# Moving the scatter of an expert unit's results into the next unit's products

## The chip, the core and the metric

The kernel runs on one core of a Trainium2 chip. The metric is the device time of one execution in microseconds (us). The engines are named as the profile names them: PE is the matrix engine (PEld its weight loads), DVE the vector engine, ACT the scalar engine, POOL the general engine, SP the queue that issues the transfers.

## What is computed

Two layers of a decoder trunk over 256 tokens of width 1024. Each layer has a mixing part (an RWKV head group and a sparse attention head group) and then a mixture of 16 experts, of which each token uses two. Only the second part is touched here. Its core, cut from the reference:

```python
h2 = rms_norm(x, norm_g[l, 1]) * (1.0 + sc2) + sh2
x = x + gate_ffn * moe_ffn(h2, router_w, router_b, exp_w_gate[l], exp_w_up[l], exp_w_down[l])

def expert_block(args):          # inside moe_ffn: xe are the tokens of expert e
    xe, e = args
    return (jax.nn.silu(xe @ w_gate[e]) * (xe @ w_up[e])) @ w_down[e]

yb = lax.map(expert_block, (xb, blk_expert)).reshape(P, D)
y = jnp.zeros((N + 1, D), h.dtype).at[slot_tok].add(yb * slot_w[:, None])
```

Each expert has 1024x512 gate weights, as many up weights and 512x1024 down weights in float32.

## The kernel before

The mixture is worked off in seven units per layer. A unit has 128 slots, shared between two experts of 64 slots (units 0, 1, 4, 5, 6), four experts of 32 (unit 2), or one of 96 and one of 32 (unit 3). A unit's products for its experts go to different column groups of the matrix engine (`tile_position` 0, 32, 64, 96: its lanes), so that neighbouring instructions of different lanes run at the same time.

The weights come in chunks of 1 MB, 96 per layer, in the order unit, matrix (gate, up, down), half of the contraction, expert. Counted from 0, unit 2 has chunks 24 to 47, unit 3 has 48 to 59, unit 4 has 60 to 71, unit 5 has 72 to 83, unit 6 has 84 to 95. `fetch` issues them on SP into a ring of 18 buffers, and a chunk can be issued when the chunk 18 places before it has been used.

The steps of a unit `i`:

- `pick` and `gather` (L1243, L1247): products of the token rows with one-hot columns bring the tokens of a pair of units into `xeA` or `xeB`; 32 products with full weights, for units 2 and 3 together, 4 and 5 together, and 6 alone.
- `prepare` (L1296, L1286, L1288, L1290): the one-hot matrix `ohT` that carries the unit's slots back to tokens, and the slots' weights `sw`.
- `hidden` (L1353): the gate products into one bank `pg`, then the up products into `pu`. For each, 8 steps of the contraction times the lanes.
- `gated` (L1306 on ACT, L1307 and L1308 on DVE): silu(gate) times up into `hb`.
- `turn` (L1315 on PE, L1317 on ACT): four transposes.
- `down` (L1364): the down products into two banks `p2[0]`, `p2[1]`, the two halves of the 1024 outputs.
- `scatter` (L274, L275, L1326, L1329), once for each half: ACT copies the half to `ys` in the reduced format, DVE writes the remainder (L275), PE multiplies both by `ohT` (eight products with full weights into `ps_rw`), DVE adds the result to `xT` (L1329). `ys` has one buffer, so the second half is copied when the first half's products have read it.

Before, unit `i`'s two scatters are issued in the program right behind `down(i)`, `pick` and `prepare(i+1)`, and a scheduler, which sets the order of each engine's queue when the kernel is built, lays them among the neighbouring instructions, those of `hidden(i+1)` among them. Ahead of the last unit's `turn` stands `rest`, a branch that is taken when an expert has more tokens than slots; every engine passes it.

Of the kernel before, what the change touches and what calls it, by code (L numbers as in the profile page):

```python
# [21 lines left out]
NK = D // 128  # L22
# [89 lines left out]
def tile_trunk(ctx: ExitStack, tc: tile.TileContext, a: dict, layers=L, dump=None):  # L112
    nc = tc.nc
    ve, ac, po, pe, sp = nc.vector, nc.scalar, nc.gpsimd, nc.tensor, nc.sync
# [183 lines left out]
    with tc.tile_pool(name="start", bufs=8, reuse_waits="tile") as start:  # L298
# [6 lines left out]
        pss = ps("sq")  # L305
# [4 lines left out]
        for ci in (2, 0, 3, 1):  # L310
            p = ps("mm")
# [7 lines left out]
            p = ps("rw")  # L319
# [8 lines left out]
    for l in range(layers):  # L328
# [740 lines left out]
        def fetch(n=0):  # L1069

            done[0] += n
            while len(loaded) < min(done[0] + len(slots), len(chunks)):
                i = len(loaded)
                e, m, r = chunks[i]
                w = slots[i % len(slots)].tile([128, 2048], F32, name="w", tag="w")
                sp.dma_start(w, a["exp"][l, expert(e), m, r])
                loaded[chunks[i]] = w
# [224 lines left out]
        def gated(p_g, p_u, sw, h):  # L1302

            for i in range(2):
                o = slice(256 * i, 256 * i + 256)
                ac.activation(h[:, o], p_g[:, o], AF.Tanh, scale=0.5)  # L1306
                ve.scalar_tensor_tensor(h[:, o], h[:, o], 1.0, p_g[:, o], op0=ALU.add, op1=ALU.mult)  # L1307
                ve.scalar_tensor_tensor(h[:, o], p_u[:, o], sw, h[:, o], op0=ALU.mult, op1=ALU.mult)  # L1308
# [10 lines left out]
        def scatter(p, cols, pss=None, store=False):  # L1319

            split(ys[:, 0], ys[:, 1], p)
            for j in range(0, len(cols), 2):
                p = ps("rw")
                for i, (d, o, ohT) in enumerate(cols[j:j + 2]):
                    for n in range(2):
                        pe.matmul(p[:, i * 256:i * 256 + 256], lhsT=ys[:, n, o:o + 128], rhs=ohT, start=(n == 0), stop=(n == 1),  # L1326
                                  skip_group_check=True)
                for i, (d, o, ohT) in enumerate(cols[j:j + 2]):
                    ve.scalar_tensor_tensor(xT[:, d, :], p[:, i * 256:i * 256 + 256], gfh[:, d:d + 1], xT[:, d, :],  # L1329
                                            op0=ALU.mult, op1=ALU.add)  # L1330
                    if store:
                        sp.dma_start(a["out"][:, d, :], xT[:, d, :])
                    if pss is not None:
                        sumsq(pss, d, xes[0][:, d, :])
# [9 lines left out]
        def hidden(i):  # L1344
            xe = xes[(i // 2) % 2]
            pg, pu = ps("mm"), ps("mm")
            for m, p in ((0, pg), (1, pu)):
                for r in range(2):
                    for k in range(4 * r, 4 * r + 4):
                        for e, o, n in lanes(i):  # L1350
                            w = loaded[e, m, r].rearrange("p (k n) -> p k n", k=4)
                            x = 128 * (i % 2) + o
                            pe.matmul(p[o:o + n, :], lhsT=xe[:, k, x:x + n], rhs=w[:, k % 4, :],  # L1353
                                      start=(k == 0), stop=(k == NK - 1), skip_group_check=True)
                    fetch(len(units[i]))
            gated(pg, pu, sws[i % 2], hs)

        def down(i, hsT):
# [56 lines left out]
        def sort():  # L1415

            key = mt([16], "key")
            ve.scalar_tensor_tensor(key, num, 16.0, C[:, C_KEY:C_KEY + 16], op0=ALU.mult, op1=ALU.add)
            t = hb[:, 512:1280].rearrange("p (a b c) -> p a b c", a=4, b=12)
            t2 = t.rearrange("p a b c -> p (a b c)")[:, 0:256].rearrange("p (a b) -> p a b", a=16)  # L1420
            ve.tensor_tensor(t2, key.unsqueeze(1).to_broadcast([128, 16, 16]), key.unsqueeze(2).to_broadcast([128, 16, 16]),
                             op=ALU.is_lt)
            rank = mt([16], "rank")
            ve.tensor_reduce(rank, t2, axis=AX.X, op=ALU.add)
            perm = hs[:, 128:320].rearrange("p (a b) -> p a b", a=12)
            ve.tensor_tensor(perm, rank.unsqueeze(1).to_broadcast([128, 12, 16]),
                             iota[:, 0:12].unsqueeze(2).to_broadcast([128, 12, 16]), op=ALU.is_equal)
            ve.tensor_mul(t[:, 0], perm, iota[:, 0:16].unsqueeze(1).to_broadcast([128, 12, 16]))
            ve.tensor_reduce(order_, t[:, 0], axis=AX.X, op=ALU.add)
            ve.tensor_copy(order, order_)  # L1430
            for x, o in ((rkp, 0), (wt, 2)):
                ve.tensor_mul(t[:, o:o + 2], x.unsqueeze(2).to_broadcast([128, 2, 12, 16]),
                              perm.unsqueeze(1).to_broadcast([128, 2, 12, 16]))
            ve.tensor_reduce(srt, t, axis=AX.X, op=ALU.add)

            ve.tensor_scalar(cap, rank, 4.5, -32.0, op0=ALU.is_lt, op1=ALU.mult)
            ve.tensor_scalar(key, rank, 11.0, 32.0, op0=ALU.is_equal, op1=ALU.mult)
            ve.scalar_tensor_tensor(cap, cap, 64.0, key, op0=ALU.add, op1=ALU.add)
            ve.tensor_sub(key, num, cap)
            ve.tensor_scalar(key, key, 0.0, None, op0=ALU.max)  # L1440
            ve.tensor_copy(over[:, 0:16], key)
            ve.tensor_reduce(rank[:, 0:1], key, axis=AX.X, op=ALU.max)
            ve.tensor_copy(over[:, 16:17], rank[:, 0:1])
# [6 lines left out]
        pick((0, 1), xes[0], lambda: [low_part(q) for q in range(1, 4)])  # L1450
        prepare(0)
        sort()
        for i in range(len(units)):
            last = i == len(units) - 1
            hidden(i)
            if last:
                if l + 1 < layers:
                    persist["win"] = {ci: load("win", l + 1, ci).rearrange("p (k n) -> p k n", k=NK) for ci in range(RA_N - 1)}
                rest(xes[1 - (i // 2) % 2])
            turn(hs, 128, hsTs[0])  # L1460
            p2 = down(i, hsTs[0])
            if last and l + 1 < layers:
                persist["win"][RA_N - 1] = load("win", l + 1, RA_N - 1).rearrange("p (k n) -> p k n", k=NK)
            if not last:
                if i % 2:
                    pick([j for j in (i + 1, i + 2) if j < len(units)], xes[((i + 1) // 2) % 2])
                prepare(i + 1)
            pss = ps("mm") if last and l + 1 < layers else None
            for n in range(2):
                scatter(p2[n], [(d, 128 * (d % 4), ohTs[i % 2]) for d in range(4 * n, 4 * n + 4)], pss,  # L1470
                        last and l + 1 == layers)
            if pss is not None:
                persist["rs"] = norm_rs(sumsq_end(pss, xes[0][:, 0, :]))
        E_.close()
# [76 lines left out]
```

## Time and profile before

| | us |
|---|---|
| three runs | 1196.7, 1196.71, 1189.7 |
| median | 1196.7 |
| profiled execution, its own time | 1189.87 |
| span of the profiled execution | 1188.1 |

| engine | busy, share of the span |
|---|---|
| PE | 90% |
| DVE | 55% |
| ACT | 34% |
| POOL | 11% |

The profiled execution is about as long as the fastest of the three runs, 6.8 us under their median. The mixture of layer 0 lies from about 380 to 617 us in the profile, that of layer 1 from about 950 us to the end, with the same pattern 571.9 us later. In the profile one product of float32 data (L1353, L1364) makes two rows of the count, so that x32 there are 16 instructions of the program; the products of the scatter and the gather (L1326, L1243) make one.

### The profile page before, as it was taken

To read this page: it belongs to the slowest core of one execution; us is meant where nothing else is said; L and a number is where in the kernel's file an instruction comes from. 1 tells how busy PE (TensorE), PEld (TensorE's weight loads), DVE (VectorE), ACT (ScalarE), POOL (GpSimd) and SP (SyncE) were. 2 spreads that over 40 slices of the span, in tenths; PEclk is the share of its full clock that TensorE was granted. 3 is DMA by queue.
4 is the path that set the end of the run, shared out by engine and by line. 5 is a ranking of instruction groups with operands and counts; after the bars stand their busy time and mean duration, and the time that the engine had idled before them with its cause. 6 is when DMAs were issued, how large, how long until landed. Compare 5 with 4: busy or idle time off the path is not lost. (4 is left out here: it accounts for less than half of the span.)

```text
span 1188.1 us, 19652 instructions
## 1 busy us (share of the span) xinstructions
PE 1068.4 (90%) x7568; PEld 688.4 (58%) x7568; DVE 653.2 (55%) x1727; ACT 402.8 (34%) x922; POOL 134.1 (11%) x196
## 2 busy tenths in 40 slices
PE   5779899998797999999968999999989799999996
PEld 2658767886696343333337777778769744333432
DVE  1799788788575322121238988886748532212222
ACT  1634434356553020101035444344655321120100
POOL 0431232310000000000023212331000000000000
PEclk9889999999798999999988899999999899999998
DMA  9755664474577999999775466433346969999991
GB/s 382 266 189 187 224 226 174 168 245 164 200 311 321 373 421 419 420 420 419 295 268 179 152 239 213 161 135 133 108 167 273 409 267 420 420 420 419 419 396 38
DMA packets 52815, 328.48 MB, mean 276 GB/s; under 512 B 5856, under 2 KB 7520, under 8 KB 18784
## 3 DMA queue, kind: packets, MB, share of 16 engines
q1 hardware_dynamic: 52416, 326.91, 70.5%
q8 instruction: 63, 1.03, 0.3%
q14 instruction: 48, 0.39, 0.1%
q10 hardware_dynamic: 288, 0.14, 0.0%
HBM read 325.98 MB, written 1.05 MB: 275 GB/s over the span
## 5 line engine op out<-in xcount | busy, mean ns | idle before, releaser
L288 PE MATMUL ps_mm<-h,w 128*128 128x256 f32 x1824 | 266.8, 295 | 16.4 <-ACT w L274 8.1
L288 PEld LDWEIGHTS ps_mm<-h,w 128*128 128x128 f32 x1824 | 233.5, 194 | 35.7 <-issue 10.1
L275 DVE TENSOR_TENSOR w<-w,w 128x1024 fp32r<-128x1024 f32 (+2 forms) x130 | 140.2, 1082 | 16.3 <-ACT w L274 16.1
L274 ACT ACTIVATE w<-w 128x1024 fp32r<-128x1024 f32 (+2 forms) x130 | 120.1, 936 | 61.4 <-PE ps_mm L288 36.7
L1353 PE MATMUL ps_mm<-w,xeA 128*64 128x512 f32 x512 | 130.1, 599 | 0.0
L1364 PE MATMUL ps_mm<-w,hb 128*64 128x512 f32 (+1 forms) x576 | 123.0, 607 | 1.7 <-DMA w<-in_exp 1.2
L225 DVE CUSTOM_DVE_ANT_0 wa<-wa,crow 128x1024 f32<-128x1024 f32 x80 | 98.3, 1229 | 1.2 <-DMA wa<-in_ada 1.0
L1353 PE MATMUL ps_mm<-w,xeB 128*32 128x512 f32 (+1 forms) x640 | 97.8, 595 | 0.0
L275 DVE TENSOR_TENSOR ys<-ps_mm,ys 128x512 fp32r<-128x512 f32 x28 | 19.2, 686 | 110.5 <-ACT ys L274 110.5
L1364 PEld LDWEIGHTS ps_mm<-w,hb 128*64 128x64 f32 (+1 forms) x576 | 36.6, 127 | 73.3 <-issue 66.3
L737 PE MATMUL ps_mm<-w,h 128*128 128x512 f32 (+1 forms) x288 | 76.2, 394 | 1.0 <-DVE w L275 0.7
L1353 PEld LDWEIGHTS ps_mm<-w,xeA 128*64 128x64 f32 x512 | 37.5, 137 | 65.6 <-issue 62.3
L1307 DVE SCALAR_TENSOR_TENSOR hb<-hb,ps_mm 128x256 f32<-128x256 f32 x28 | 11.8, 421 | 99.7 <-ACT hb L1306 99.7
L274 ACT ACTIVATE ys<-ps_mm 128x512 fp32r<-128x512 f32 x28 | 16.7, 596 | 131.2 <-PE ps_mm L1364 101.3
L1308 DVE SCALAR_TENSOR_TENSOR hb<-ps_mm,sw,hb 128x256 f32<-128x256 f32 x28 | 12.3, 480 | 86.5 <-PE ps_mm L1353 86.5
L1329 DVE SCALAR_TENSOR_TENSOR xT<-ps_rw,gfh,xT 128x256 f32<-128x256 f32 x112 | 46.6, 478 | 23.3 <-PE ps_rw L1326 23.3
L1353 PEld LDWEIGHTS ps_mm<-w,xeB 128*32 128x32 f32 (+1 forms) x640 | 26.0, 115 | 51.8 <-issue 48.4
L737 PEld LDWEIGHTS ps_mm<-w,h 128*128 128x128 f32 x288 | 48.1, 198 | 12.5 <-issue 2.7
L1326 PEld LDWEIGHTS ps_rw<-ohT,ys 128*128 128x128 f32 x224 | 30.6, 188 | 38.8 <-ACT ys L274 19.4
L1243 PEld LDWEIGHTS ps_rw<-OH,h 128*128 128x128 f32 x256 | 35.7, 208 | 29.7 <-issue 23.8
L288 PE MATMUL ps_mm<-y,w 128*128 128x256 f32 x384 | 49.8, 294 | 3.2 <-ACT w L274 3.0
L288 PEld LDWEIGHTS ps_mm<-y,w 128*128 128x128 f32 x384 | 48.9, 200 | 3.9 <-ACT w L274 3.8
(458 smaller groups left out, 1512.9 us busy)
## 6 DMA issues: line engine op xcount, KB each, us to landing
w<-in_exp SPq DMA_DIRECT2D x192, 1024.0 KB, 19.7
w<-in_win SPq DMA_DIRECT2D x40, 1024.0 KB, 4.9
wa<-in_ada SPq DMA_DIRECT2D x80, 512.0 KB, 4.5
w<-in_ada SPq DMA_DIRECT2D x8, 1024.0 KB, 14.1
w<-in_cmp SPq DMA_DIRECT2D x8, 1024.0 KB, 6.0
w<-in_up SPq DMA_DIRECT2D x8, 1024.0 KB, 7.1
w<-in_out SPq DMA_DIRECT2D x8, 1024.0 KB, 5.9
row<-in_row SPq DMA_DIRECT2D x2, 780.0 KB, 7.3
```

The costliest lines, as they stand in the source:

```text
L225: ve.tensor_tensor_reduce(w, w, crow, 1.0, 0.0, op0=ALU.mult, op1=ALU.add, accum_out=mod[:, o:o + 1])
L274: ac.activation(hi, x, AF.Copy)
L275: e.tensor_sub(lo, x, hi.bitcast(F32))
L288: pe.matmul(out, lhsT=w2[i][:, k, :], rhs=x2[j][:, k, :], start=(k == ks[0] and not (i or j)), stop=(k == ks[-1] and j == 1), skip_group_c ...
L737: pe.matmul(p[tt][:, 0:n], lhsT=h2[j][:, k, tt * 128:tt * 128 + 128], rhs=w2[i][:, k - k0, :], start=(k == 0 and not (i or j)), stop=(k == ...
L1243: pe.matmul(p[:, k * 256:k * 256 + n], lhsT=h[:, tt, kk_ * 128:kk_ * 128 + 128], rhs=OH[:, tt, 0:n], start=(i == 0 and tt == 0), stop=(i = ...
L1307: ve.scalar_tensor_tensor(h[:, o], h[:, o], 1.0, p_g[:, o], op0=ALU.add, op1=ALU.mult)
L1308: ve.scalar_tensor_tensor(h[:, o], p_u[:, o], sw, h[:, o], op0=ALU.mult, op1=ALU.mult)
L1326: pe.matmul(p[:, i * 256:i * 256 + 256], lhsT=ys[:, n, o:o + 128], rhs=ohT, start=(n == 0), stop=(n == 1), skip_group_check=True)
L1329: ve.scalar_tensor_tensor(xT[:, d, :], p[:, i * 256:i * 256 + 256], gfh[:, d:d + 1], xT[:, d, :], op0=ALU.mult, op1=ALU.add)
L1353: pe.matmul(p[o:o + n, :], lhsT=xe[:, k, x:x + n], rhs=w[:, k % 4, :], start=(k == 0), stop=(k == NK - 1), skip_group_check=True)
L1364: pe.matmul(p2[n][o:o + m, :], lhsT=hsT[:, 2 * r + g, o:o + m], rhs=w[:, g, n * 512:n * 512 + 512], start=(r + g == 0), stop=(r + g == 2), ...
```

## The change

The scatter of unit `i` is no longer issued behind `down(i)`. Its two halves are put on a list, and `hidden(i+1)` takes one from it behind its gate products and the other behind its up products. `tc.issue_after(mm.ins)` orders the half's products on PE behind the last of the products just issued. The last unit's halves are issued where they were.

```diff
                         for e, o, n in lanes(i):
                             w = loaded[e, m, r].rearrange("p (k n) -> p k n", k=4)
                             x = 128 * (i % 2) + o
-                            pe.matmul(p[o:o + n, :], lhsT=xe[:, k, x:x + n], rhs=w[:, k % 4, :],
-                                      start=(k == 0), stop=(k == NK - 1), skip_group_check=True)
+                            mm = pe.matmul(p[o:o + n, :], lhsT=xe[:, k, x:x + n], rhs=w[:, k % 4, :],
+                                           start=(k == 0), stop=(k == NK - 1), skip_group_check=True)
                     fetch(len(units[i]))
+                if behind:
+                    with tc.issue_after(mm.ins):
+                        behind.pop(0)()
             gated(pg, pu, sws[i % 2], hs)
...
+        behind = []
         for i in range(len(units)):
...
             pss = ps("mm") if last and l + 1 < layers else None
-            for n in range(2):
-                scatter(p2[n], [(d, 128 * (d % 4), ohTs[i % 2]) for d in range(4 * n, 4 * n + 4)], pss,
-                        last and l + 1 == layers)
+
+            def half(n, i=i, p2=p2, pss=pss, store=last and l + 1 == layers):
+                scatter(p2[n], [(d, 128 * (d % 4), ohTs[i % 2]) for d in range(4 * n, 4 * n + 4)], pss, store)
+
+            behind += [lambda n=n, h=half: h(n) for n in range(2)]
+            if last:
+                while behind:
+                    behind.pop(0)()
```

The line of `down` becomes L1367. The order on PE from `down(2)` on, before (`ohT_4153` is unit 2's; `OH`, `h_4107` and `h_4108` belong to the gather for units 4 and 5):

```order
L1364 MATMUL ps_mm<-w,hb 32x512 x30
L1326 MATMUL ps_rw<-ohT_4153,ys 128x256 x8
L1353 MATMUL ps_mm<-w,xeB 32x512
L1326 MATMUL ps_rw<-ohT_4153,ys 128x256
L1353 MATMUL ps_mm<-w,xeB 32x512 x2
L1326 MATMUL ps_rw<-ohT_4153,ys 128x256 x7
L1243 MATMUL ps_rw<-OH,h_4107 128x256 x2
L1243 MATMUL ps_rw<-OH,h_4108 128x256
L1353 MATMUL ps_mm<-w,xeB 32x512 x13
```

The same place in the changed kernel:

```order
L1367 MATMUL ps_mm<-w,hb 32x512 x30
L1353 MATMUL ps_mm<-w,xeB 32x512 x32
L1326 MATMUL ps_rw<-ohT_4153,ys 128x256 x8
L1353 MATMUL ps_mm<-w,xeB 32x512 x32
L1326 MATMUL ps_rw<-ohT_4153,ys 128x256 x8
L1315 MATMUL ps_tr<-C,hb 128x128 x4
```

Unit 3's gate and up products are now whole blocks of 32, each with one half of unit 2's scatter behind it, and the gather for units 4 and 5 has left them. It went into `down(3)`, where the scheduler cut the 32 down products into 6, 10, 6 and 10:

```order
L1315 MATMUL ps_tr<-C,hb 128x128 x4
L1367 MATMUL ps_mm<-w,hb 32x512 x6
L1243 MATMUL ps_rw<-OH,h_4107 128x256
L1367 MATMUL ps_mm<-w,hb 32x512 x10
L1243 MATMUL ps_rw<-OH,h_4107 128x256
L1243 MATMUL ps_rw<-OH,h_4108 128x256 x2
L1243 MATMUL ps_rw<-OH,h_4107 128x256 x2
L1243 MATMUL ps_rw<-OH,h_4108 128x256 x2
L1243 MATMUL ps_rw<-OH,h_4107 128x256 x2
L1243 MATMUL ps_rw<-OH,h_4108 128x256 x2
L1367 MATMUL ps_mm<-w,hb 32x512 x6
```

Before, these down products were one run with two transposes in it. The gather for unit 6 moves likewise from `hidden(5)` into and behind `down(5)`. On SP the issues keep their order.

## Rows read from the trace of the kernel before

**Rows 1.** The profile page: busy share of the engines, transfer rate in 40 slices.

```profile
PE 1068.4 (90%) x7568; PEld 688.4 (58%) x7568; DVE 653.2 (55%) x1727; ACT 402.8 (34%) x922; POOL 134.1 (11%) x196
...
GB/s 382 266 189 187 224 226 174 168 245 164 200 311 321 373 421 419 420 420 419 295 268 179 152 239 213 161 135 133 108 167 273 409 267 420 420 420 419 419 396 38
```

**Rows 2.** Windows: length; PE, PEld, DVE, ACT, POOL busy; granted clock, DMA share, GB/s.

```profile
469.90:507.60 37.70, 36.11 (x248) 13.60 (x247) 7.91 (x19) 6.74 (x14) 0.00 (x0) 1.00 1.01 420
...
593.30:599.80 6.50, 0.00 (x0) 0.01 (x1) 0.88 (x2) 0.00 (x0) 1.40 (x6) 0.75 0.86 325
```

**Rows 3.** SP's issues from 466.3 us; landing of the issue at 566.87; SP's waits, 400 to 600.

```profile
466.52 100.68 SPq L1076 DMA_DIRECT2D w<-in_exp  x41
...
w<-in_exp SPq DMA_DIRECT2D x1, 1024.0 KB, 19.7
...
SPq L1076 <- DMA w<-in_exp: 86.5, 46, 2.6
```

**Rows 4.** Timeline of PE, unit 3: start, duration, line, count, idle before and its releaser.

```profile
466.44 3.62 PE L1364 MATMUL ps_mm<-w,hb 128*32 128x512 f32 x20 [0.59 <-DMA w<-in_exp]
469.99 0.51 PE L1326 MATMUL ps_rw<-ohT,ys 128*128 128x256 f32 x2
470.68 0.97 PE L1326 MATMUL ps_rw<-ohT,ys 128*128 128x256 f32 x6 [0.17 <-DVE ys L275]
471.58 1.05 PE L1353 MATMUL ps_mm<-w,xeB 128*32 128x512 f32 x2
...
475.56 0.62 PE L1243 MATMUL ps_rw<-OH,h 128*128 128x256 f32 x3 [0.62 <-DVE xT L1329]
...
480.21 1.06 PE L1353 MATMUL ps_mm<-w,xeB 128*32 128x512 f32 x6
...
497.48 0.89 PE L1315 MATMUL ps_tr<-C,hb 128*128 128x128 f32 x4 [0.58 <-DVE hb L1308]
498.39 1.92 PE L1364 MATMUL ps_mm<-w,hb 128*32 128x512 f32 x12
500.24 0.44 PE L1286 MATMUL ps_tr<-C,OW 128*128 128x128 f32 x2
500.61 7.05 PE L1364 MATMUL ps_mm<-w,hb 128*32 128x512 f32 x52
507.59 0.50 PE L1326 MATMUL ps_rw<-ohT,ys 128*128 128x256 f32 x2
```

**Rows 5.** Timeline of PE, unit 0: half a gather, an uncut run of down products.

```profile
382.76 2.18 PE L1243 MATMUL ps_rw<-OH,h 128*128 128x256 f32 x16
...
400.53 7.09 PE L1364 MATMUL ps_mm<-w,hb 128*64 128x512 f32 x32
```

**Rows 6.** Timeline of PE, the ends of units 4, 5 and 6; then layer 1's unit 6.

```profile
536.82 0.50 PE L1326 MATMUL ps_rw<-ohT,ys 128*128 128x256 f32 x2
...
574.77 0.50 PE L1326 MATMUL ps_rw<-ohT,ys 128*128 128x256 f32 x2
...
579.33 13.95 PE L1353 MATMUL ps_mm<-w,xeB 128*64 128x512 f32 x62
...
1151.20 13.95 PE L1353 MATMUL ps_mm<-w,xeB 128*64 128x512 f32 x62
1169.34 0.63 PE L1315 MATMUL ps_tr<-C,hb 128*128 128x128 f32 x4 [4.20 <-issue]
```

**Rows 7.** Timelines of DVE and ACT behind `down(3)`: the second half's copies.

```profile
509.17 0.60 ACT L274 ACTIVATE ys<-ps_mm 128x512 fp32r<-128x512 f32 x1 [1.67 <-PE ps_rw L1326]
510.51 0.68 DVE L275 TENSOR_TENSOR ys<-ps_mm,ys 128x512 fp32r<-128x512 f32 x1
511.90 1.66 DVE L1329 SCALAR_TENSOR_TENSOR xT<-ps_rw,gfh,xT 128x256 f32<-128x256 f32 x4 [0.71 <-PE ps_rw L1326]
```

**Rows 8.** Windows about the wait for the weights, and behind the branch.

```profile
463.00:466.40 3.40, 2.85 (x12) 0.67 (x7) 0.00 (x0) 0.00 (x0) 0.00 (x0) 1.00 1.01 419
...
596.70:600.10 3.40, 0.28 (x2) 0.32 (x3) 0.00 (x0) 0.00 (x0) 0.00 (x0) 0.50 0.70 280
```

## The prediction

> **What bounds the kernel now.** I read the page first: PE is busy for 90% of the span, and the transfer rate stands at about 420 GB/s in two plateaus, the two mixtures of experts [rows 1]. The windows of one mixture come next, since the change touches nothing else. In unit 3 PE is busy for 36.1 of 37.7 us while the transfers run at 420 GB/s without a pause [rows 2]: two things are nearly full at once, so a faster PE may merely wait for weights. Third, the weight queue: from 466.52 us on SP issues 41 chunks in 100.7 us, held back 46 times by an earlier transfer [rows 3], so the stream sets its own pace. The last chunk, 95, is issued at the end of that row (567.20 less its own 0.33, 566.87) and lands 19.7 us later, at 586.6. Fourth, the timeline of PE. It tells where the two meet: at 466.44 PE waits for weights, at the last chunk of unit 2, chunk 47 [rows 4]. So 48 chunks land in 586.6 - 466.4 = 120.2 us, one per 2.50 us, whatever PE does. A unit of 12 chunks is 30.0 us of stream; whoever makes PE faster than that finds the stream.
>
> **Where PE loses time behind that point.** Unit 2's scatter and unit 3 take from 469.99 to 507.59, 37.6 us [rows 4], and not mostly by waiting. Visible waits are 0.17 for the DVE's copy, 0.62 for a bank that DVE has yet to empty, 0.58 for `gated` [rows 4]. More is lost in busy time: one gate product alone (x2) holds PE for 1.05 us, and three (x6) for 1.06, although 10 products in four lanes take 3.62 and an uncut run of 16 in two lanes 7.1 [rows 4, 5]. A lane group costs about 0.9 us, full or not. Every scatter or gather piece laid between the lanes therefore pays for empty lanes, and the busy share hides it.
>
> **The change, part by part.** The profiled execution took 1189.87 us; I sum against that.
>
> 1. *Ahead of unit 2's end: nothing.* Units 0 to 2 get faster too, but chunk 47 lands at 466.4 either way, and PE waits for it today [rows 4]. The stream hides all of it.
>
> 2. *Unit 3 runs at the stream's pace.* The gate and up products are whole blocks now, 7.1 us each [rows 5] for 4 chunks, against 10.0 us of stream. The second half of up needs chunk 55: 466.4 + 8 x 2.50 = 486.4. Behind that come half a block, 3.6 (the duration of x20, which has as many lane groups to fill) [rows 4], and half a scatter: 6 of its products start 0.90 us before the next row (470.68 to 471.58), so 8 cost 1.2 [rows 4]. `turn` is 0.9 (497.48 to 498.39) [rows 4]; its wait of 0.58 goes, because the scatter stands in it. So `down(3)` starts at 492.1. It is cut into 6, 10, 6, 10; the rows x12 (1.85 to its successor) and x20 (3.6) are just these pieces, together 11.0 [rows 4]. The gather, 32 products at 2.18/16 = 0.136, is 4.4 [rows 5]; transposes 0.4 [rows 4]. End: 507.9, against 507.59 today. Unit 3 brings nothing: what the lanes win is waited away, and the gather that filled the wait now comes behind it.
>
> 3. *Unit 4* needs 2 x (7.1 + 1.2) + 0.9 = 17.5 up to its `down`, which keeps its one cut and takes 9.2, as 498.39 to 507.59 [rows 4]. End 534.6, today 536.82 [rows 6]: 2.2 ahead. Its chunks are early.
>
> 4. *Unit 5.* The second half of its up products starts at 534.6 + 8.3 + 3.6 = 546.5 and needs chunk 79: 466.4 + 32 x 2.50 = 546.4. They just meet. `down(5)` starts at 552.1; cut down products 11.0, gather 4.4, transposes 0.4: end 567.9, today 574.77 [rows 6]: 6.9 ahead. Today this unit's gather cuts its gate and up products.
>
> 5. *Unit 6*: 16.6 us, to 584.5. Today the up products end at 579.33 + 13.95 = 593.28 [rows 6]: **8.8 us per layer**. The pause before the branch, 6.5 us here [rows 2] and 4.20 in layer 1 [rows 6], follows PE's last product and stays; chunk 95 (586.6) is there before the last `down` wants it. Behind that both kernels have the same work.
>
> 6. *The new dependencies* I cost at nothing. A half's products now wait, in PE's queue, for `ys`; behind them stand the next block, `turn` and `down`. The first half is copied during 7.1 us of gate products. The second half's copy needs the first half's products to end, then ACT 0.60, four DVE additions 1.66 and DVE 0.68 [rows 7], 2.9 in sequence and less in part side by side, during 7.1 us of up products. Margin about 4 us; without cover it costs up to 2.9 per unit. `p2` is held longer, but its banks are wanted only by the next `down`. SP's issues keep their order and slots come free earlier or at the same time, so the stream does not starve.
>
> 7. *The clock.* PE will now wait more often: two chunks take 5.0 us of stream and 3.6 of products, so about 1.4 us at each of five or six places between 461 and 487 us. Today's wait there (0.59 us without a product) stays at the granted clock 1.00 (2.4 GHz), while the 6.5 us pause at the branch ends at 0.50 (1.2 GHz) [rows 8]. I am nearer to the first row, so I take no loss; the second is the upper end. The Trainium skill speaks against this change here ("TensorE: Matmul & The Clock Gate", section "HAM oscillation — how this bites in real kernels"): it tells of a kernel whose bursts of products, each followed by a wait for a transfer, fell to the low clock again and again. By that the time would come out as in the first rival.
>
> **Sum.** Layer 1 repeats the pattern 571.87 us later (579.33 and 1151.20) [rows 6], so 2 x 8.8 = 17.6 and 1189.87 - 17.6 = **1172.3 us** on the scale of the profiled execution. The runs' median is 6.8 higher, which would make 1179. I name **1174**, since one of three runs lay on the low value and the profiled execution too.
>
> **Rivals.**
>
> - *Slower: the waits for weights drop the clock.* Place: unit 2's `down` to unit 3's `down`, both layers. At 1.2 GHz work takes twice as long, so x us spent there lose x/2. As 8.8 us per layer are to be lost before the change costs anything, it decides from about 18 us at the low clock in each layer. If it held from 487 to 530, 43 us, that loses 21.5, net -12.7 per layer: 1215. For it: five waits close together. Against: each is a quarter of the pause that dropped it. Chance 5%.
> - *Only a small gain.* The waits on `ys` or on a bank return inside the blocks, as the 0.62 us before the gather shows can happen [rows 4], or the stream lands 3 us later and takes all of units 4 and 5 with it. With 3 to 5 us less per layer: 1178 to 1182 on the profiled scale, up to 1189 on the median's. Chance 19%.
> - *Nothing moves*, because each engine's queue is as before where it counts. The order of PE shows otherwise; the gain would have to be eaten by cut `down` runs in units 3 and 5 (each 1.8 over the uncut 9.2). 1190 to 1197. Chance 4%.
> - *More than I think:* blocks overlap with the end of `down` where no full-width product parts them, 1 us per unit: 1164. Chance 7%.
>
> The forecast keeps 65%, from 1168 to 1180. The range 1164 to 1188 takes in most of the second rival and leaves out the clock, the nothing and the tails. A change under 1%, 12 us about the median of 1196.7, can't be told from none here. Faster needs 1184.7: forecast, the larger gain and a third of the small one, 0.77; same 0.17; slower 0.06.
>
> **What would show it.** Right: `L1353` in whole blocks of 7.1 us; PE waits on `w<-in_exp` between 461 and 487 us, about 1.4 each; no idle before `L1315`; `down(3)` ending near 508 and the last scatter of unit 6 near 584.5; clock 1.00 throughout. Wrong: idle before L1326 put down to ACT or DVE (step 6), clock 0.50 in unit 3 (step 7), gaps in the stream between 466 and 567, or unit 5 far from 568.

## The result, and the profile after

The changed kernel's median is 1178.68 us over six runs (1174.73 to 1179.4), against 1193.4 for the kernel before beside it (1189.7 to 1196.71). The ratio is 0.9866, 95% interval 0.9839 to 0.9893: 1.3% faster. The profiled execution took 1174.77 us (span 1173.0) against 1189.87 (span 1188.1); 1172.3 was worked out for it, 1174 named.

Where the 15.1 us of span come from shows best when each layer's mixture is cut out: from its first gate product to PE's last product ahead of the branch's pause. Windows of layer 0 and layer 1, before (length; busy time of PE, PEld, DVE, ACT, POOL; granted clock, DMA share, GB/s):

```profile
381.76:593.28 211.52, 204.60 (x1079) 78.55 (x1078) 51.30 (x128) 31.05 (x68) 0.00 (x0) 1.00 0.94 388
952.53:1165.15 212.62, 205.71 (x1079) 78.84 (x1078) 51.15 (x128) 31.05 (x68) 0.00 (x0) 0.99 0.93 386
```

The same two stretches of the changed kernel:

```profile
383.56:585.61 202.05, 194.47 (x1079) 78.62 (x1078) 49.06 (x127) 30.14 (x68) 0.00 (x0) 1.00 0.98 404
946.58:1148.34 201.76, 194.65 (x1079) 78.06 (x1078) 48.98 (x127) 30.15 (x68) 0.00 (x0) 1.00 0.98 404
```

Read the first row against the first. PE executes 1079 products (rows of the profile's count) both times, at the granted clock 1.00 (2.4 GHz) both times, and is **busy** for 10.1 us less (204.60 to 194.47). Its idle time is not less but more: 6.9 and 7.6. So the gain of 9.5 us here and 10.9 in layer 1 (where the window before stands at 0.99, which cost it 1.1 us at its start: `turn` of unit 0 came 19.0 us behind the first gate product, 17.9 in layer 0) shows as busy time alone: products that no longer leave lanes empty. The waits only changed their names. PE's waits between the same ends in layer 0, changed kernel (engine, line, releaser: us in total, times, longest):

```profile
PE ps_mm L1353 <- DMA w<-in_exp: 3.9, 4, 1.4
PE ps_mm L1367 <- DMA w<-in_exp: 1.8, 3, 0.6
PE ps_mm L1367 <- ACT hb L1317: 1.3, 5, 0.3
```

5.7 us are waits for weights now (0.6 before), and none is put down to `ys` or `xT`: the copies of a half are covered.

The timeline of PE through unit 3 answers to [rows 4] (`hidden` is L1353 as before, `down` L1367; start, duration, line, shape, count, idle before and releaser):

```profile
468.07 2.76 PE L1367 MATMUL ps_mm<-w,hb 128*32 128x512 f32 x18 [0.59 <-DMA w<-in_exp]
...
473.06 3.64 PE L1353 MATMUL ps_mm<-w,xeB 128*32 128x512 f32 x32 [1.37 <-DMA w<-in_exp]
478.05 3.62 PE L1353 MATMUL ps_mm<-w,xeB 128*32 128x512 f32 x26 [1.34 <-DMA w<-in_exp]
481.60 1.20 PE L1326 MATMUL ps_rw<-ohT,ys 128*128 128x256 f32 x8
...
488.01 3.62 PE L1353 MATMUL ps_mm<-w,xeB 128*32 128x512 f32 x26 [0.79 <-DMA w<-in_exp]
491.56 1.21 PE L1326 MATMUL ps_rw<-ohT,ys 128*128 128x256 f32 x8
492.61 0.60 PE L1315 MATMUL ps_tr<-C,hb 128*128 128x128 f32 x4
...
507.56 1.34 PE L1243 MATMUL ps_rw<-OH,h 128*128 128x256 f32 x9
...
509.06 7.09 PE L1353 MATMUL ps_mm<-w,xeA 128*64 128x512 f32 x32
```

The scatter stands whole behind each block (x8, 1.2 us), `turn` follows without a wait, PE waits 0.6 to 1.4 us for chunks in four places, and the gather now stands in and behind `down(3)` (32 products between 495 and 508.7 us, the last nine shown). Unit 6 and the branch, against [rows 6]:

```profile
584.40 1.21 PE L1326 MATMUL ps_rw<-ohT,ys 128*128 128x256 f32 x8
592.18 1.08 PE L1315 MATMUL ps_tr<-C,hb 128*128 128x128 f32 x4 [6.57 <-issue]
593.31 9.60 PE L1367 MATMUL ps_mm<-w,hb 128*64 128x512 f32 x32
```

The pause is as long as before (6.57 against 6.5 [rows 2]). In all: the mixtures give 9.5 + 10.9 = 20.4 us; the start, with the same work, took 1.8 longer (383.56 against 381.76); `turn` and the last `down` behind the two pauses took 2.6 longer; the pauses and the stretch between the layers 0.9 longer. 20.4 - 1.8 - 2.6 - 0.9 = 15.1. The 1.8 can't be put down to the change: two executions of the changed kernel differ by 4.7 us in their start (last section).

### The profile page after: what moved, and what is told of

The parts are those of the page before. It is cut to its first block, busy times and chain, and to the rows that moved or that the text cites. A ratio compares the mean times of both kernels' runs of the same rounds, so it can differ in the third digit from the quotient of the medians.

```text
span 1173.0 us, 19674 instructions
## 1 busy us (share of the span) xinstructions
PE 1049.9 (90%) x7568; PEld 688.0 (59%) x7568; DVE 650.0 (55%) x1727; ACT 401.1 (34%) x922; POOL 134.0 (11%) x196
## 5 line engine op out<-in xcount | busy, mean ns | idle before, releaser
L288 PEld LDWEIGHTS ps_mm<-h,w 128*128 128x128 f32 x1824 | 232.1, 193 | 37.0 <-issue 10.4
L275 DVE TENSOR_TENSOR w<-w,w 128x1024 fp32r<-128x1024 f32 (+2 forms) x130 | 140.1, 1081 | 16.4 <-ACT w L274 16.2
L1367 PE MATMUL ps_mm<-w,hb 128*64 128x512 f32 (+1 forms) x576 | 138.9, 613 | 6.3 <-DMA w<-in_exp 3.5
L1353 PE MATMUL ps_mm<-w,xeA 128*64 128x512 f32 x512 | 120.3, 595 | 0.4 <-DMA w<-in_exp 0.4
L1353 PE MATMUL ps_mm<-w,xeB 128*32 128x512 f32 (+1 forms) x640 | 89.5, 595 | 7.0 <-DMA w<-in_exp 7.0
L1367 PEld LDWEIGHTS ps_mm<-w,hb 128*64 128x64 f32 (+1 forms) x576 | 39.5, 127 | 83.7 <-issue 66.1
L1353 PEld LDWEIGHTS ps_mm<-w,xeA 128*64 128x64 f32 x512 | 37.9, 137 | 69.7 <-issue 66.4
L1353 PEld LDWEIGHTS ps_mm<-w,xeB 128*32 128x32 f32 (+1 forms) x640 | 26.6, 115 | 61.0 <-issue 45.9
L1308 DVE SCALAR_TENSOR_TENSOR hb<-ps_mm,sw,hb 128x256 f32<-128x256 f32 x28 | 12.3, 480 | 74.2 <-PE ps_mm L1353 74.2
L1317 ACT ACTIVATE hb<-ps_tr 128x256 f32<-128x256 f32 x28 | 9.7, 382 | 123.1 <-PE ps_tr L1315 122.9
L1243 PEld LDWEIGHTS ps_rw<-OH,h 128*128 128x128 f32 x256 | 34.8, 207 | 20.4 <-issue 19.7
```

The costliest lines, as they stand in the source:

```text
L275: e.tensor_sub(lo, x, hi.bitcast(F32))
L288: pe.matmul(out, lhsT=w2[i][:, k, :], rhs=x2[j][:, k, :], start=(k == ks[0] and not (i or j)), stop=(k == ks[-1] and j == 1), skip_group_c ...
L1243: pe.matmul(p[:, k * 256:k * 256 + n], lhsT=h[:, tt, kk_ * 128:kk_ * 128 + 128], rhs=OH[:, tt, 0:n], start=(i == 0 and tt == 0), stop=(i = ...
L1317: ac.activation(hsT[:, 2 * i:2 * i + 2].rearrange("p f s -> p (f s)"), p[:, 0:2 * parts], AF.Copy)
L1353: mm = pe.matmul(p[o:o + n, :], lhsT=xe[:, k, x:x + n], rhs=w[:, k % 4, :], start=(k == 0), stop=(k == NK - 1), skip_group_check=True)
L1367: pe.matmul(p2[n][o:o + m, :], lhsT=hsT[:, 2 * r + g, o:o + m], rhs=w[:, g, n * 512:n * 512 + 512], start=(r + g == 0), stop=(r + g == 2), ...
```

## The experiments

My theory is that of the prediction: a piece of full-width work laid between the lanes costs what it leaves of them empty, the gain is that cost, and the weight stream takes back what units 0 to 3 gain. The rivals: the waits on copies and on `gated` are what counts; the stream hides nothing; the missing microseconds were lost behind the pause. Below, "a mixture" is the stretch of the windows above, given for layer 0 and layer 1: 211.5 and 212.6 before, 202.1 and 201.8 after. It is the better measure: the start ahead of it differs between executions of one program.

**Scatter in pieces, between lane groups and inside them.** Each half's scatter comes in four pieces; the number of pieces and their order are the same, and only the count of products at which they are laid differs: by at most one in the units with two experts of 64, by two to five in the units with four lanes of 32. (The second run's expectation says one product; the lines above are what ran.)

```diff
+            count, at = [0, 0], {2: (6, 8, 12, 14), 4: (12, 16, 24, 28)}[len(list(lanes(i)))]   # pieces_even
+            count, at = [0, 0], {2: (5, 8, 11, 14), 4: (9, 14, 19, 26)}[len(list(lanes(i)))]    # pieces_odd
...
+                            count[m] += 1
+                            if behind and count[m] in at:
+                                with tc.issue_after(mm.ins):
+                                    behind.pop(0)()
```

> The changed kernel with each half's scatter not in one piece behind a block but in four, laid into the block between whole lane groups (8 pieces per unit in place of 2). Theory (a piece costs what it leaves of a lane group empty): at these places next to nothing, hidden(4)'s gate block 7.1 us and 1.2 us of scatter; by a count of lane groups about 2.5 us per layer behind the changed kernel, 1 to 8 us in all. Rival A (what counts is the number of pieces, each with a price of its own, wherever it lies): the same time as pieces_odd. Rival B (only PE's waits on the copies count, and the pieces now have less time for theirs): idle time ahead of L1326, put down to DVE, about 1 us per half.

> As pieces_even, with the pieces laid inside a lane group instead, one product of the block earlier or later; the number of pieces, their order and what they wait for are the same. Theory: each piece opens a lane group that is only filled in part, about 0.9 us for two lanes or four, in units 4 and 6 a block of 7.1 us takes 9 to 10.7; by the count of lane groups some 19 us per layer behind the changed kernel, less where the stream hides it (units 0 to 3), so 20 to 39 us slower than the changed kernel in all, and slower than the kernel before. Rival (the gain of the change is the waits on copies and on gated that it covers): within 3 us of pieces_even.

Measured: 1177.38 us (two runs) between lane groups, ratio to the kernel before 0.9862 (0.9833 to 0.989); 1216.54 inside them, ratio 1.019 (1.0106 to 1.0274). The mixtures are 204.5 and 204.7, against 222.6 and 223.6. Unit 6 between lane groups:

```profile
569.23 2.79 PE L1375 MATMUL ps_mm<-w,xeB 128*64 128x512 f32 x12
571.95 0.50 PE L1331 MATMUL ps_rw<-ohT,ys 128*128 128x256 f32 x2
572.38 1.08 PE L1375 MATMUL ps_mm<-w,xeB 128*64 128x512 f32 x4
...
573.82 1.94 PE L1375 MATMUL ps_mm<-w,xeB 128*64 128x512 f32 x8
```

and inside them:

```profile
583.85 2.79 PE L1375 MATMUL ps_mm<-w,xeB 128*64 128x512 f32 x10
586.57 0.50 PE L1331 MATMUL ps_rw<-ohT,ys 128*128 128x256 f32 x2
587.00 1.93 PE L1375 MATMUL ps_mm<-w,xeB 128*64 128x512 f32 x6
```

This is the price in its plainest form, in rows of the profile: six take 1.93 us and eight take 1.94; ten take 2.79 and twelve 2.79. With two lanes the time goes up in steps of 0.86 us per four rows (two products of the program, one in each lane), and whoever cuts inside a step pays for all of it. No wait on `ys` appears in PE's waits of either. By the whole mixture the cuts inside cost 18.0 and 18.9 us per layer, where the count gave some 17. Theory confirmed, rival A (a price per piece) and rival B (waits) fallen.

**The scatter uncut, but not covered.** Both halves ahead of the next unit's gate products, as one block.

```diff
             xe = xes[(i // 2) % 2]
+            after = ExitStack()
+            if behind:
+                while behind:
+                    behind.pop(0)()
+                after.enter_context(tc.issue_after(persist["sc"].ins))
...
```

> The changed kernel with both halves of a unit's scatter ahead of the next unit's gate products, as one block: no product of the next unit stands between lanes cut by it, but its waits for the copies are uncovered, as is gated's. Theory (cuts and waits both count): the waits return, 0.2 and 1.4 to 2.2 us for the two copies and 0.6 for gated, 2.4 us per unit, of which units 0 to 3 are hidden by the stream; 4 to 9 us per layer behind the changed kernel, 8 to 18 in all, so about where the kernel before stands or up to 7 us ahead of it. Rival (only the cuts count): within 2 us of the changed kernel. Rival (only the waits count): as slow as the kernel before.

Measured: 1202.0 us (five runs), ratio 1.0082 (1.0047 to 1.0117): slower than the kernel before. The mixtures are 216.6 and 217.0, so 14.6 and 15.2 per layer behind the changed kernel, where I had expected 4 to 9. PE's waits in layer 0 are the expected ones:

```profile
PE ps_rw L1326 <- DVE xT L1329: 5.2, 10, 0.7
PE ps_tr L1315 <- DVE hb L1308: 3.0, 5, 0.7
PE ps_rw L1326 <- DVE ys L275: 2.0, 10, 0.2
```

Idle time is 12.0 us, 4.4 more than in the changed kernel. But the busy time in the same window is back at 204.63, the value of the kernel before, although no scatter cuts a lane any more. Most of that is the clock: the window stands at 0.97 (0.96 in layer 1) in place of 1.00, with four stretches of 6 us at 0.72 (from 421, 451, 550 and 592 us), which lose some 1.7 us each, 7 in all; none of it was in my expectation. In the other 3 to 4 us are cuts, those of the gather, which the scheduler put back into `hidden(3)` and `hidden(5)`: 553.15 to 577.0 for the gate and up products of unit 5 that take two blocks of 7.1 when whole. And unit 3 shows no wait for weights at all, so the stream hid none of the new waits, as I had assumed it would. Three costs stand side by side in this run, so it does not tell what the uncut scatter alone is worth. It raised the question that became the main one: is it the scatter's cuts or the gather's that the change took away?

**The gather alone.** The kernel before, its scatter cut as it was, and only the gather for units 4 to 6 laid behind the half blocks of `hidden(3)` and `hidden(5)`.

```diff
+                    if parts:
+                        with tc.issue_after(mm.ins):
+                            parts.pop(0)()
                     fetch(len(units[i]))
...
+            if i % 2 and i > 1:
+                pick([j for j in (i + 1, i + 2) if j < len(units)], xes[((i + 1) // 2) % 2], None, parts)
             hidden(i)
```

> The kernel before with its scatter where it was, cut between the lanes, and one thing altered: the gather for units 4 and 5 and for unit 6 is laid in four pieces behind the four half blocks of hidden(3) and of hidden(5), between whole lane groups. Theory A (most of what the change brought is not the scatter's own cuts but the gather's, which the scheduler let cut the gate and up products of units 3 and 5 and no longer does): turn to turn, unit 3 goes from 41.1 to about 34 us, where the weights bind, and unit 5 from 38.0 to about 32; 9 to 13 us per layer, as much as the change or more. Rival B (the scatter's cuts were the cost): 0 to 4 us per layer.

The same edit on the changed kernel:

> The changed kernel with the gather for units 4 and 5 and for unit 6 laid in four pieces behind the half blocks of hidden(3) and hidden(5), where PE waits for weights, in place of being laid by the scheduler into down(3) and down(5). Theory: the gather then fills waits of 1.3 us each and down(3) and down(5) stay whole but for the transposes; 3 to 8 us per layer less than the changed kernel, 6 to 16 in all. Rival (the weights bind unit 3 and unit 5 in either case, so the time comes back as longer waits for weights): within 2 us per layer.

and the changed kernel itself beside them:

> The changed kernel itself beside the two others, for the comparison on one chip: 1174 to 1180 us.

Measured, on one chip: 1173.4, 1169.83 and 1177.47 us (four runs each); ratios to the kernel before 0.9807 (0.9753 to 0.986), 0.9786 (0.9733 to 0.9838) and 0.9837 (0.9781 to 0.9893). The windows of layer 0's mixture, in that order:

```profile
388.74:589.45 200.71, 194.80 (x1079) 76.31 (x1078) 51.35 (x128) 30.57 (x68) 0.00 (x0) 1.00 0.98 404
```

```profile
382.22:581.84 199.62, 193.55 (x1079) 79.93 (x1078) 49.89 (x127) 30.02 (x68) 0.00 (x0) 1.00 0.98 404
```

```profile
388.23:590.63 202.40, 194.66 (x1079) 79.30 (x1078) 49.15 (x127) 30.19 (x68) 0.00 (x0) 1.00 0.98 404
```

With the scatter left in its cuts, the gather's place alone takes the mixture from 211.5 to 200.7 (layer 1: 212.6 to 200.5): 10.8 and 12.1 us, slightly more than the whole change, the size that theory A gave. But theory A also says that the change's own gain is mostly the gather's, and that the rows do not bear out. Windows of units 4, 5 and 6 in layer 0, each to the end of the unit's `down` and of the gather behind it (unit 6 to the end of the mixture), first with the gather moved, then the changed kernel:

```profile
509.86:539.10 29.24, 28.11 (x123) 10.43 (x119) 7.42 (x18) 2.73 (x6) 0.00 (x0) 1.00 1.01 420
539.10:570.93 31.83, 30.63 (x152) 13.23 (x151) 7.08 (x17) 5.62 (x14) 0.00 (x0) 1.00 1.01 419
570.93:589.45 18.52, 18.03 (x82) 6.90 (x80) 5.39 (x12) 1.36 (x3) 0.00 (x0) 1.00 1.01 421
```

```profile
509.06:535.43 26.37, 26.11 (x125) 10.35 (x126) 8.14 (x21) 3.42 (x8) 0.00 (x0) 1.00 1.01 420
535.43:569.23 33.80, 33.15 (x148) 14.45 (x143) 6.56 (x15) 5.06 (x13) 0.00 (x0) 1.00 1.01 419
569.23:585.61 16.38, 16.38 (x81) 6.42 (x80) 4.74 (x12) 1.93 (x5) 0.00 (x0) 1.00 1.02 420
```

| us, layer 0 | units 0 to 3 | unit 4 | unit 5 | unit 6 |
|---|---|---|---|---|
| before [rows 4, 6] | 125.8 | 29.2 | 38.0 | 18.5 |
| gather moved, scatter cut | 121.1 | 29.2 | 31.8 | 18.5 |
| changed kernel | 125.5 | 26.4 | 33.8 | 16.4 |

The moved gather earns in units 3 and 5 alone. The change earns 2.9 us in unit 4 and 2.1 in unit 6, where no gather stood among the lanes before: at least 5.0 of its 9.5 us are the scatter's. In unit 5, 4.2 us, the two can't be told apart. Layer 1 repeats units 4 to 6 within 0.5 us. So the two edits take away different costs that happen to be about as large. Nor does the moved gather spare gate and up products alone: `down(3)` and `down(5)` take 7.5 us each in place of 9.2: the transposes in them now cut the rows at another place, in `down(5)` into 16 and 16 (3.65 and 3.66 us) in place of 4 and 28 (1.93 and 7.08).

Adding the uncut scatter to the moved gather brings another 1.1 and 1.3, with 4.3 us of waits for weights in place of 0.6. Half of unit 5's gate block in the kernel before, cut by the gather (timeline of PE):

```profile
546.38 1.07 PE L1353 MATMUL ps_mm<-w,xeA 128*64 128x512 f32 x2
...
548.64 3.65 PE L1353 MATMUL ps_mm<-w,xeA 128*64 128x512 f32 x14
```

and with the gather moved and the scatter as before:

```profile
548.27 3.65 PE L1370 MATMUL ps_mm<-w,xeA 128*64 128x512 f32 x16
551.86 1.11 PE L1273 MATMUL ps_rw<-OH,h 128*128 128x128 f32 x8
```

16 rows, in 2 and 14, take 4.7 us; together they take 3.65. Turn to turn, unit 5 takes 38.0 us before, 33.1 here, 27.6 in the changed kernel (where the gather went into `down(5)` and so into unit 6's 39.3 in place of 35.2); unit 3 takes 41.1, 37.4 and 38.2. I had expected 32 and 34 with the gather moved; the weights do not bind unit 3 there, as no wait for them stands behind unit 2's `down`. The kernel with both edits is the fastest of those that leave nothing out; its mixtures are 2.8 and 3.6 us shorter than those of the changed kernel beside it, at or just under the low end of what I expected (3 to 8).

**Half the weights.** The transfer of every chunk cut to half, in the kernel before and in the changed one; the products use the half twice (those lines are left out here).

```diff
-                sp.dma_start(w, a["exp"][l, expert(e), m, r])
+                sp.dma_start(w[:, 0:1024], a["exp"][l, expert(e), m, r][:, 0:1024])
```

> The kernel before, with each chunk of the experts' weights transferred to half (its first 1024 columns) and these used twice, so half of the experts' weights is left out. PE's products are as many as before. Theory (unit 3 and half of unit 5 run at the pace of the weight stream, 2.50 us per chunk): with 1.25 us per chunk PE never waits for weights between 461 and 580 us, and the last scatter of unit 6 ends 8 to 16 us per layer earlier than the 593.3 and 1165.2 us of before. Rival (weights don't bind, lane cuts and waits alone set the time): within 3 us of before per layer.

> The changed kernel with the same halved transfers (half of the experts' weights left out). Theory: units 0 to 3 now give their gain too, so that the distance to half_before is 11 to 18 us per layer, 22 to 36 in all, where the change gave 15 with whole transfers; PE's waits on weights in units 2 to 5 go from 1.4 us each to nothing. Rival (the stream hides nothing, and the gain of 15 us is all there is): half_after is 13 to 17 us ahead of half_before. Second rival (PE's clock sets the time, not its waits): the clock without these waits is 1.00 as with them, so no change at all.

Measured: 1145.15 and 1120.54 us (two runs each); ratios to the kernel before 0.9608 (0.958 to 0.9636) and 0.9402 (0.9374 to 0.9429). The change is worth 24.6 us here, inside the 22 to 36 of the theory, near its low end, and PE waits for no weights. Layer 0's mixture, the kernel before and the changed one:

```profile
383.79:571.39 187.60, 185.46 (x1079) 73.61 (x1078) 51.13 (x128) 30.99 (x68) 0.00 (x0) 1.00 0.61 219
```

```profile
383.70:560.39 176.69, 174.77 (x1079) 72.47 (x1078) 48.90 (x127) 30.08 (x68) 0.00 (x0) 1.00 0.65 233
```

Not a clean test, though: with lighter transfers the scheduler also chose another order, in which the gather cuts no lanes in either kernel. In the changed one it stands whole behind `down` (`539.82 4.01 ... x32`), in the kernel before a quarter of it beside `turn` and the rest behind `down`. So the 24 to 25 us that both lost of layer 0's mixture, where I had allowed the kernel before 16 at most, are not the weights' alone. Read as it is, the pair tells what the scatter's own cuts cost when neither gather nor weights interfere: 10.9 us in layer 0, 10.7 of it busy time, and 11.9 in layer 1 (188.65 and 176.74, from 919.31 us), where the kernel before lost some 1.1 us to a low clock at the start. That is at the low end of the 11 to 18 per layer that I had expected.

**Half of 16 chunks.** So I asked of the stream alone, with PE's order kept in layer 0.

```diff
-                sp.dma_start(w, a["exp"][l, expert(e), m, r])
+                c = 1024 if 12 <= i < 28 else 2048; sp.dma_start(w[:, 0:c], a["exp"][l, expert(e), m, r][:, 0:c])
...
```

> The changed kernel with chunks 12 to 27 of each layer transferred to half and this half used twice (a half of 16 of the 96 chunks' weights is left out); PE's order in layer 0 stays as it is but for one pair of transposes, so this asks of the stream alone. 16 x 1.25 = 20 us of stream fewer ahead of chunk 47. Theory (units 2 to 5 run at the stream's pace): the waits for weights, 5.7 us in layer 0, go, and the mixture of layer 0 up to the last scatter of unit 6 goes from 202.1 to 195 to 198 us; its unit 3 falls most, from 38.2 to about 33 us turn to turn. Rival (the waits are only moved cover, and PE's work is the bound): 200 us or more.

Measured: 1171.78 us (two runs), ratio 0.9798 (0.9728 to 0.9868); the mixtures 197.5 and 198.0, unit 3 33.7 us turn to turn: in the expected range, so the weights do bind the changed kernel, by 4.5 us in layer 0. But 4.2 us of waits for weights are left, where I had them all gone. Of 20 us of stream only 4.5 came out, all of it ahead of unit 3: the wait for chunk 47 ends 80.0 us behind the first gate product in place of 84.5, and from the end of unit 2's `down` on the mixture takes 113.9 us in both kernels. Windows from 395 and from 455 us:

```profile
395.00:420.00 25.00, 24.36 (x111) 7.89 (x108) 3.40 (x8) 2.15 (x6) 0.00 (x0) 1.00 0.84 289
...
455.00:500.00 45.00, 40.51 (x292) 14.96 (x287) 9.59 (x23) 4.19 (x10) 0.00 (x0) 1.00 1.01 419
```

The transfers stood below their 420 GB/s just when they had less to move (289 here, 422 in the same stretch of the changed kernel). That the ring's slots were full then, so that a stream that is early can't run far ahead of PE, is likely but not shown: SP's issues waited 25.6 us for products of L1353 (386 to 590 us), but 43.9 us in the changed kernel (383 to 590). By 455 us the stream is at its pace again, and PE waits as before.

**Without the branch.** The line that calls `rest` is left out, before and after.

```diff
-                rest(xes[1 - (i // 2) % 2])
```

> The kernel before without the branch for tokens above an expert's capacity (none here, so nothing of the result is left out on this input). Theory: the pauses of 6.5 and 4.2 us go down to gated's 0.6 to 1.5 us, and the last down runs at the granted clock 1.00 (7.1 us for x32 in place of 8.3): 9 to 12 us less than before in all.

> The changed kernel without the same branch. Theory (the 3.2 us of the gain that are missing in the span were given back behind the pause, where the last down now takes 9.6 us in place of 8.3): 12 to 15 us less than the changed kernel, and 17 to 20 us ahead of no_branch_before, against 15.1 between the profiled executions with the branch. Rival (they were lost elsewhere, in the start or the end): still 14 to 16 ahead of no_branch_before.

Measured: 1193.94 us (eight runs), ratio 0.9978 (0.9937 to 1.0019), and 1176.31 (two runs), ratio 0.987 (0.9827 to 0.9912). Against my expectation neither total moved. The place itself did as told (changed kernel without the branch):

```profile
592.56 0.60 PE L1315 MATMUL ps_tr<-C,hb 128*128 128x128 f32 x4
593.42 7.14 PE L1367 MATMUL ps_mm<-w,hb 128*64 128x512 f32 x32 [0.26 <-ACT hb L1317]
```

No pause, and the last `down` takes 7.14 us in place of 9.60 (8.27 before). Pause, `turn` and `down` together fall from 15.9 and 13.7 to 8.6 and 8.6 in the kernel before, from 17.2 and 15.5 to 7.8 and 7.8 in the changed one. The mixtures are worth as much as with the branch: 211.8 and 213.8 against 202.4 and 203.0. The rest was lost elsewhere: the stretch from layer 0's last scatter to layer 1's first gate product takes 355.1 and 351.9 us, in place of 343.4 and 343.7. PE has as many products there to within one, but is busy for 6.3 and 4.6 us longer, at a granted clock of 0.93 and 0.95 in place of 0.95 and 0.97, and idle for 5.4 and 3.5 us longer. From unit 6 on the scheduler lays the program out otherwise; whether that is the cause was not tested. And in these two executions the start took 5.6 and 6.8 longer. Between the two kernels lie 17.6 us, as the theory wanted (17 to 20), but with intervals of some 5 us on each side that alone tells little; the rows at the place tell it: in these executions 2.6 us of the gain were given back behind the pauses.

**Both halves behind the up products.**

```diff
-                if behind:
+                while behind and m:
```

> The changed kernel with both halves behind the up products, one after the other, before turn and down. Theory: the first half is covered, the second waits in PE's queue for its copy, which can't begin before the first half's products end: up to 2.9 us less what turn and the first down products fill in; if down products are laid ahead of it, they are cut and cost 0.5 to 1 us each instead. 1 to 3 us per unit, of which units 4 to 6 count: 3 to 9 us per layer behind the changed kernel, 6 to 18 in all. Rival (the second copy is no wait, as ACT and DVE are fast enough): within 2 us of it.

Measured: 1181.74 us (four runs), ratio 0.9894 (0.9834 to 0.9953); the mixtures 206.2 and 205.4, so 4.1 and 3.6 per layer behind the changed kernel, in the expected range. In all it is 3.1 us behind, under the 6 to 18 expected; a part came back in the pauses, which are 5.0 and 4.0 us long here in place of 6.6 and 4.7. The second half is laid into the next `down` and cuts it (525.90 and 526.90 below), but unit 6 starts only 1.7 and 1.5 us later for it. The other 2.4 and 2.1 us come in unit 6, whose `turn` and `down` stand behind the branch: nothing is laid ahead of the second half, and it waits for its copies.

```profile
525.90 1.07 PE L1367 MATMUL ps_mm<-w,hb 128*64 128x512 f32 x2 [0.47 <-ACT hb L1317]
526.90 0.38 PE L1326 MATMUL ps_rw<-ohT,ys 128*128 128x256 f32 x1
...
585.87 0.36 PE L1326 MATMUL ps_rw<-ohT,ys 128*128 128x256 f32 x1 [0.75 <-ACTq L1376]
...
587.16 1.63 PE L1326 MATMUL ps_rw<-ohT,ys 128*128 128x256 f32 x6 [0.21 <-DVE ys L275]
```

PE's busy time is within 0.9 us of the changed kernel's (195.3 and 194.6); what grew is its idle time, by 3.3 and 3.7 us.

## Why the prediction was right, step by step

- **Step 1, nothing ahead of unit 2's end: right.** The wait for chunk 47 ends 84.5 us behind the first gate product (468.07 less 383.56), before 84.7 (466.44 [rows 4] less 381.76).
- **Step 2, unit 3 brings nothing: right in the end, less so in the way.** On the scale of before (1.80 us off the start) unit 4's first product starts at 507.3; I had 507.9. Its waits were 1.37, 1.34 and 0.79 us, with three of 0.5 to 0.7 ahead of them in `down(2)`, not five or six of 1.4. (The 46 waits that I put into 100.7 us of the stream are those of 400 to 600 us [rows 3]; 41 of them, 76.8 us, lie in it, and the reading stands.)
- **Steps 3 to 5: the mechanism right, each gain a little small.** On the same scale unit 4 ends 3.2 us ahead (535.4 less 1.8, against 536.82 [rows 6]; I had 2.2), unit 5 7.3 (6.9), unit 6 9.5 (8.8), in layer 1 10.9. The last products of `down(4)` overlap with the first of unit 5, as the rival "more" said, for about 1 us. Chunk 79 is just met: its wait is 0.39 us.
- **Step 6, the copies cost nothing: right**, as no wait on `ys` shows; that this needs the cover is seen where the second half has none.
- **Step 7, no loss of clock: right.** The window of layer 0's mixture stands at 1.00, with four waits of 0.6 to 1.4 us between 468 and 488. The Trainium skill ("TensorE: Matmul & The Clock Gate", section "HAM oscillation — how this bites in real kernels") tells of bursts of products with waits for transfers that fell to the low clock each time; this trace doesn't show that here. The kernel with the uncovered scatter did lose clock among shorter waits (last section), so that rival was no empty one.
- **"Behind that both kernels have the same work": true, and yet the step that failed.** `turn` and the last `down` took 9.33 and 9.46 us before, 10.66 and 10.77 now. It is the clock behind the pause, which I had costed as equal. Windows over layer 0's `turn` and `down`, before and now:

```profile
599.82:609.15 9.33, 9.28 (x37) 3.13 (x37) 0.06 (x1) 1.46 (x4) 0.00 (x0) 0.81 0.26 87
```

```profile
592.18:602.84 10.66, 10.61 (x36) 3.42 (x36) 0.06 (x1) 1.45 (x4) 0.00 (x0) 0.71 0.24 81
```

  Without the pause both kernels take 7.9 to 8.0 us at 1.00. Whether the change itself makes this stretch longer is not shown: the second execution of the changed kernel took 10.04 and 11.34, the other kernels with the branch lie between 9.1 and 12.3, and the kernel before was profiled once.

The sum was 17.6 us; the mixtures gave 20.4, and 5.3 went elsewhere (1.8 start, 2.6 behind the pauses, 0.9 between), so 15.1. That the total came out so near is in part luck: two misses of opposite sign. The medians lie 14.7 us apart (1193.4 and 1178.68).

What the sum did not tell is how scatter and gather share the cost. I priced lane groups by what cuts them, scatter and gather alike, and followed the built order. The experiments show that moving the gather alone brings about as much (10.8 and 12.1 us) in units 3 and 5, that the change earns about half of its gain in units 4 and 6, where only the scatter stood, and that both edits together bring 11.9 and 13.4 and not the sum, with the weights next in line. What the scatter's cuts alone cost with whole weights and the gather in its old place, no run shows; with half the weights it is 10.9 in layer 0. That the changed kernel moved its gather at all is a by-product of the scheduler's.

Open: why a change of the transfers' size or of the branch makes the scheduler lay the gather and the stretch between the layers otherwise was not tried. Nor was it settled why 20 us less of stream brought only 4.5.

## What to carry to other kernels

Where products share the array in lanes, count them in the steps that fill it (here one product in each of two lanes, four rows of the profile, 0.86 us): a piece of full-width work laid at a step's edge costs only itself, inside a step it costs the rest of the step, and the busy share hides that. Before crediting a moved operation with a gain, look what else the scheduler moved with it; cut out the stretch that the change touches, unit by unit, and compare busy time at equal instruction counts: two edits that bring the same total need not remove the same cost. A wait for weights is a good place for such pieces: the order that laid the gather there was the fastest here of those that leave nothing out.

## What the runs showed of the hardware

- The same program starts at different speeds. In two executions of the changed kernel the first gate product starts at 383.56 and at 388.23 us. 4.7 us of that are lost by 32 us, where the same 16 products take 1.92 in one and 3.64 in the other:

```profile
19.83 1.92 PE L315 MATMUL ps_mm<-w,csx 128*32 128x512 f32 x16
```

```profile
20.65 3.64 PE L315 MATMUL ps_mm<-w,csx 128*32 128x512 f32 x16
```

  The window of 12 to 30 us shows a granted clock of 1.00 in both, so that column does not catch it.
- Among short waits between single products the clock fell in some places and not in others. In the kernel with the uncovered scatter, four waits of 0.2 to 0.7 us among the products of one scatter left it at 1.00 at 518 to 530 us, but at 0.76 at 549 to 556, and the gate and up products behind the next such row took 15.65 us in place of 13.95:

```profile
518.00:530.00 12.00, 10.56 (x50) 4.56 (x50) 4.60 (x10) 1.15 (x2) 0.00 (x0) 1.00 1.02 422
...
549.00:556.00 7.00, 5.74 (x21) 2.98 (x22) 3.92 (x9) 0.60 (x1) 0.00 (x0) 0.76 1.01 418
...
592.00:598.00 6.00, 6.00 (x24) 1.98 (x24) 1.66 (x4) 0.00 (x0) 0.00 (x0) 0.72 0.57 236
```

  It fell at four of the six scatters of layer 0 and at five of layer 1's six, which by the granted clock lost some 7 and 8 us. What sets these places apart is not shown.

- Behind the branch's pause `turn` and the last `down` took between 9.1 and 12.3 us over the kernels and layers, and 7.9 to 8.0 without the pause: a pause of 4 to 8 us cost some 1 to 4 us more behind it, and the longer pause not the more (4.1 us and 12.3 in one layer, 8.2 us and 10.4 in another).
